# Gates as tanh, the decay loaded in its own layout, sums of squares added up on TensorE

## The chip, the cores and the metric

The kernel runs on one core of a Trainium2 chip. Its engines work side by side, each on its own list of instructions in order: TensorE (PE, with its weight load PEld), VectorE (DVE), ScalarE (ACT), GpSimd (POOL) and SyncE (SP), which here only issues DMAs. The metric is the device time of one execution in microseconds (us), as the median of several runs.

## What is computed

One layer of a hybrid decoder on 1024 tokens of 1024 features in float32. A combined projection of the normalised input feeds three mixers (retention, Mamba-2 SSD, gated linear attention), whose outputs are merged by learned gates; an MLP follows. What the change touches:

```python
proj = h @ w_in                                  # h = rmsnorm(x); columns for all mixers and gates
# SSD, 8 chunks of 128 tokens, 16 heads of 64, state 128; a_cs = cumsum(a) in a chunk
l_mat  = exp(where(causal, a_cs[l] - a_cs[m], -inf))
y_diag = einsum(cb, l_mat, xs)                   # within the chunk
y_off  = einsum(cc, prev_states, exp(a_cs))      # from the chunks before
y = y_diag + y_off + x * d_skip
sy = group_rmsnorm(y * silu(sz), ssd_norm_w, 2)
...
g_ret, g_ssd, g_gla = split(sigmoid(mg + merge_b), 3)
merged = g_ret * ret_out + g_ssd * ssd_out + g_gla * gla_out
x = x + merged @ w_out
```

## The kernel before

Large products are made of matmuls of 128 x 128 weights with 128 x 512 activations. Each float32 operand is split in a high part and a remainder (`whi` by a cast on ScalarE, line 156, `wlo` by a subtraction on VectorE, line 157), and `acc3` (line 159) adds three products for each pair, its matmul being line 164. Most products use a seven-product block scheme: `run_set` makes a set of weights out of seven units of 12 matmuls, with `us` (lines 360, 366) as partial results. Of the 34 sets of the combined projection the last 12 are the merge gates. `e_gate` (line 481) takes a finished bank of them, adds the partial result if there is one (line 486, VectorE), applies the sigmoid with the bias column `mb_c` (line 487, ScalarE) and stores the gate to DRAM (line 489, SyncE).

The mixers run between the units of these sets: `merge` (line 949) takes a unit from the sets, then as many mixer steps as are due. Nine gate sets, 63 units, are woven with the four `ssd_mixer` runs (line 686) of 8 chunks each, 32 chunks and 72 steps in all. The call is line 1041; it runs from about 565 to 840 us. The order in which each engine's list ends up is set by the framework's scheduler, which places instructions as their inputs and buffers come free.

A chunk of the SSD mixer has two stages. `load_in` (line 697) fetches the conv outputs `xin` (line 699) and the cumulated decays `ab`, spread over all partitions (line 701), one chunk ahead. `stage_a` transposes `xin` on TensorE (lines 713 to 715), makes `xs` and `xd` (lines 718 on) and the masked scores `cbm` (line 726) on VectorE and `bt` on ScalarE (line 724). The inter-chunk decay `eb` is the exponential of `ab`, picked out by head in two halves of 64 partitions (line 732), for every chunk but the first. Four Relus (line 734) and an exponential (line 736) on ScalarE and a product on VectorE (line 737) make the intra-chunk decay. `stage_b` forms the skip product `y` on GpSimd (line 745), multiplies on TensorE (lines 750, 754, 758), sums up on VectorE (lines 767 to 771, with `eb` at 769), stores `y` (line 772), squares it on ScalarE (line 774) and adds its two halves on GpSimd (line 775). `stat` (line 777), two chunks later, sums the squares over the partitions by a one-column fp32 matmul with ones (line 779) and copies the result to `ssq` (line 780). `ssd_rows` then makes the scales out of `ssq` (GpSimd power, line 177) and transposes them (line 805).

The short-lived tiles `xs`, `xd`, `eb`, `y` and `ysq` share one ring of nine buffers, `w1m` (line 704). Later, `load_o` (line 1064) loads the mixers' outputs and scales them by the norm weights `nw_c` (lines 1077, 1081), and `branch_part` (line 1090) multiplies them by the output weights and the product by the loaded gate (line 1107), 48 times, before the branches are added up.

Of the kernel before, what the change touches and what calls it, by code (L numbers as in the profile page):

```python
# [10 lines left out]
F32 = mybir.dt.float32  # L11
F32R = mybir.dt.float32r
I32 = mybir.dt.int32
AF = mybir.ActivationFunctionType
ALU = mybir.AluOpType
# [3 lines left out]
P = 128  # L19
# [7 lines left out]
SH, SP, SG = 16, 64, 2  # L27
# [84 lines left out]
def block_kernel(ctx, tc, i, out):  # L112
    nc = tc.nc
    V, S, G, PE = nc.vector, nc.scalar, nc.gpsimd, nc.tensor

    const = ctx.enter_context(tc.tile_pool(name="const", bufs=1))
# [15 lines left out]
    nw_c = cols[:, 0:16]  # L132
    mb_c = cols[:, 16:40]
# [3 lines left out]
    nw2_c = cols[:, 62:70]  # L137
    d_c = cols[:, 70:78]
    cw_c = [cols[:, 78 + 12 * j:90 + 12 * j] for j in range(4)]
    nhalf = const.tile([P, 16], F32, name="nhalf")  # L140
    V.memset(nhalf, -0.5)

# [338 lines left out]
    def e_gate(b, d0):  # L481
        def emit(n, par, ps, other):
            d = d0 + n
            r = ev.tile([P, 512], F32, name="gt", tag="w2k")
            if other is not None:
                V.tensor_tensor(out=r, in0=ps, in1=other, op=ALU.add)
            S.activation(out=r, in_=ps if other is None else r, func=AF.Sigmoid,
                         bias=mb_c[:, 8 * b + d:8 * b + d + 1])
            nc.sync.dma_start(out=gate_d[b][d].rearrange("p (j q t) -> q p j t", q=2, t=P)[par],
                              in_=r.rearrange("p (j t) -> p j t", t=P))  # L490
        return emit
# [194 lines left out]
    def ssd_mixer(g, f4):  # L686
        R = SH // SG // 2
# [9 lines left out]
        def load_in(c):  # L697
            xin = sp.tile([P, 6, P], F32, name="xin", bufs=3)
            nc.sync.dma_start(out=xin, in_=st_d[g][c][:, 4 * f4:4 * f4 + 6])
            ab = sp.tile([P, R, P], F32, name="ab", bufs=3)  # L700
            nc.sync.dma_start(out=ab, in_=acs_d[c * SH + h0:c * SH + h0 + R, :].partition_broadcast(P))
            ins[c] = xin, ab

        def w1m(name, shape):
            return sp.tile(shape, F32, name=name, tag="w1m", bufs=9)

        def stage_a(c):
            if c + 1 < NT:
                load_in(c + 1)
            xin, ab = ins.pop(c)  # L710
            pt = ptp.tile([P, 512], F32, name="tp", tag="tp")
            for j in range(2):
                PE.transpose(out=pt[:, j * P:(j + 1) * P], in_=xin[:, sx + j, :], identity=ident)
            PE.transpose(out=pt[:, 256:384], in_=xin[:, sb, :], identity=ident)
            PE.matmul(out=pt[:, 384:512], lhsT=xin[:, sb, :], rhs=xin[:, sb + 1, :], start=True, stop=True)
            ptv = pt[:, 0:256].rearrange("p (h d) -> p h d", h=R)
            xs = w1m("xs", [P, R, SP])
            V.tensor_tensor(out=xs, in0=ptv, in1=hb(dt, c), op=ALU.mult)
            xd = bt = eb = None
            if c + 1 < NT:  # L720
                xd = w1m("xd", [P, R, SP])
                V.tensor_tensor(out=xd, in0=ptv, in1=hb(dtd, c), op=ALU.mult)
                bt = sp.tile([P, P], F32, name="bt", bufs=2)
                S.copy(out=bt, in_=pt[:, 256:384])
            cbm = sp.tile([P, P], F32, name="cbm", bufs=2)
            V.tensor_tensor(out=cbm, in0=pt[:, 384:512], in1=tri, op=ALU.mult)
            if c > 0:
                eb = w1m("eb", [P, 2, P])
                av = ab.rearrange("p (k f) t -> p f k t", f=2)
                for f in range(2):  # L730
                    rs = slice(f * SP, (f + 1) * SP)
                    S.activation(out=eb[rs], in_=av[rs, f], func=AF.Exp)
            for h in range(R):
                S.activation(out=ab[:, h, :], in_=ab[:, h, :], func=AF.Relu, scale=-1.0,
                             bias=acs[:, c, h0 + h:h0 + h + 1])
            S.activation(out=ab, in_=ab, func=AF.Exp, scale=-1.0)
            V.tensor_tensor(out=ab, in0=ab, in1=cbm.unsqueeze(1).broadcast_to([P, R, P]), op=ALU.mult)
            live[c] = (xin, ab, xs, xd, bt, eb)

        def stage_b(c):  # L740
# [31 lines left out]
            nc.sync.dma_start(out=o_d[2 + g][c // 4][:, 2 * f4:2 * f4 + 2, c % 4, :], in_=y)  # L772
            sq = w1m("ysq", [P, 2, P])
            S.activation(out=sq, in_=y, func=AF.Square)
            G.tensor_tensor(out=sq[:, 0], in0=sq[:, 0], in1=sq[:, 1], op=ALU.add)

            def stat():
                ps = ptp.tile([P, 512], F32, name="tp", tag="tp")
                PE.matmul(out=ps[:, 0:1], lhsT=sq[:, 0], rhs=ones[:, 0:1], start=True, stop=True)
                V.tensor_copy(out=ssq[:, f4, g * NT + c:g * NT + c + 1], in_=ps[:, 0:1])  # L780
            return stat

# [281 lines left out]
    def load_o(h, res, order):  # L1064
        rsy = []
        for kt in order:
# [5 lines left out]
            nc.sync.dma_start(out=raw.rearrange("p (c t) -> p c t", c=4), in_=o_d[b][h][:, k])  # L1072
            hi = bp.tile([P, 512], F32R, name="ohi", tag="ohi", bufs=16)
            lo = bp.tile([P, 512], F32R, name="olo", tag="olo", bufs=16)
            nw = nw_c[:, kt:kt + 1]
            if b in (2, 3):
                V.scalar_tensor_tensor(out=raw, in0=raw, scalar=nw, in1=rsy[b - 2].rearrange("p c t -> p (c t)"),
                                       op0=ALU.mult, op1=ALU.mult)
# [11 lines left out]
    def branch_part(h, b, o, last=False):  # L1090
        first = (0, 4, 12)[b]
        ws = None
        for d in range(KD):
# [10 lines left out]
                c0 = n * P + (512 * (d % 2) if b != 1 else 0)  # L1104
                pairs.append(((ws[0][:, c0:c0 + P], ws[1][:, c0:c0 + P]), o[k]))
            acc3(ps, pairs)
            V.tensor_tensor(out=gt, in0=ps, in1=gt, op=ALU.mult)
            if b == 0:
                accs[d] = gt
            else:  # L1110
# [268 lines left out]
```

## Time and profile before

| | |
|---|---|
| runs | 1908.94, 1909.88, 1905.97 us; median 1908.94 |
| profiled execution | 1909.4 us; span from first to last instruction 1907.6 us |
| busy in the span | PE 1866.1 us, DVE 1175.6, ACT 892.7, POOL 199.9 |
| mean granted TensorE clock | 0.993 of full speed |
| SSD stretch, 565 to 840 us | PE 264.29 of 275.00 us, ACT 233.37, DVE 196.43 |

The profile is of one execution. Busy time counts an engine's instructions; an engine's standing time is put down to the instruction that it waited for. The granted clock is that of TensorE alone: 1.00 is 2.4 GHz, 0.50 is 1.2 GHz, and what lies between is a mean over a stretch with both.

### The profile page before, as it was taken

Reading aid. Unit: us, or ns where it says so; the run is one execution under the profiler, and the core shown is the slowest. Engines: PE = TensorE matmul, PEld = TensorE weight load, DVE = VectorE, ACT = ScalarE, POOL = GpSimd, SP = SyncE. Lnnn points to the kernel's source line nnn. Section 1 sums busy time; section 2 is a strip of 40 time slices with the busy share of each in tenths; the row PEclk is TensorE's granted clock in tenths of the full one; section 3 lists DMA queues with packets and bytes.
Section 4 is the critical chain, followed back from the end, with each engine's and each line's share of the span. In section 5 each row is a group of like instructions: output and inputs, shape, how many; then the busy total and the mean of one; then the engine's idle time right before and its main releaser. Section 6 shows DMA issues by size and latency. Waiting matters only on the chain. (4 is left out here: it accounts for less than half of the span.)

```text
span 1907.6 us, 25681 instructions
## 1 busy us (share of the span) xinstructions
PE 1866.1 (98%) x9396; PEld 1538.6 (81%) x9396; DVE 1175.6 (62%) x1921; ACT 892.7 (47%) x1568; POOL 199.9 (10%) x247
## 2 busy tenths in 40 slices
PE   8999999999999999999899999999999999999998
PEld 8977778888887777777788989988888888888886
DVE  6867767668557677765877456584555434444444
ACT  7522333345449879876764123454444422111213
POOL 0011100001211112211322031000000000000003
PEclk9999999999999999999999999999999999999999
DMA  6434434234655555538667543542323362332222
GB/s 213 148 113 147 128 105 127 89 111 146 192 176 157 150 170 162 174 96 300 195 209 270 187 155 124 208 166 94 122 99 110 122 231 90 104 94 89 91 73 90
DMA packets 179342, 278.03 MB, mean 146 GB/s; under 512 B 13168, under 2 KB 114576, under 8 KB 172560
## 3 DMA queue, kind: packets, MB, share of 16 engines
q1 hardware_dynamic: 178640, 275.48, 45.4%
q8 instruction: 74, 1.21, 0.3%
q10 hardware_dynamic: 576, 0.92, 0.1%
q14 instruction: 52, 0.43, 0.1%
HBM read 193.43 MB, written 78.72 MB: 143 GB/s over the span
## 5 line engine op out<-in xcount | busy, mean ns | idle before, releaser
L156 ACT CAST whi<-raw 128x1024 fp32r<-128x1024 f32 (+1 forms) x230 | 240.6, 1048 | 494.2 <-PE mm L164 464.1
L157 DVE TENSOR_TENSOR wlo<-raw,whi 128x1024 fp32r<-128x1024 f32 (+1 forms) x230 | 293.8, 1278 | 130.6 <-ACT whi L156 123.4
L164 PE MATMUL mm<-ht,whi 128*128 128x512 f32 x1104 | 353.9, 401 | 2.5 <-DVE us L360 2.5
L164 PEld LDWEIGHTS mm<-ht,whi 128*128 128x128 f32 x1104 | 206.0, 189 | 52.8 <-DVE us L360 4.2
L164 PE MATMUL mm<-ht,wlo 128*128 128x512 f32 x552 | 219.7, 399 | 0.0
L164 PE MATMUL mm<-whi,al 128*128 128x512 f32 x512 | 202.5, 396 | 0.0
L164 PE MATMUL mm<-whi,ah 128*128 128x512 f32 x512 | 202.5, 395 | 0.0
L164 PE MATMUL mm<-wlo,ah 128*128 128x512 f32 x512 | 202.5, 395 | 0.0
L1323 DVE TENSOR_TENSOR x<-mm,x 128x512 f32<-128x512 f32 x128 | 88.2, 689 | 159.2 <-PE mm L164 159.2
L164 PE MATMUL mm<-he,whi 128*128 128x512 f32 x560 | 182.7, 404 | 0.2
L164 PE MATMUL mm<-ht,w 128*128 128x512 f32 x552 | 138.2, 397 | 0.0
L164 PEld LDWEIGHTS mm<-ht,wlo 128*128 128x128 f32 x552 | 104.1, 189 | 25.0
L164 PEld LDWEIGHTS mm<-he,whi 128*128 128x128 f32 x560 | 104.9, 190 | 23.9 <-ACT us L366 0.3
L164 PEld LDWEIGHTS mm<-ht,w 128*128 128x128 f32 x552 | 103.2, 188 | 24.6
L360 DVE TENSOR_TENSOR us<-mm,us 128x512 f32<-128x512 f32 x92 | 63.4, 689 | 90.7 <-PE mm L164 90.4
L164 PEld LDWEIGHTS mm<-whi,al 128*128 128x128 f32 x512 | 96.2, 188 | 23.4
L164 PEld LDWEIGHTS mm<-whi,ah 128*128 128x128 f32 x512 | 96.2, 188 | 23.3
L164 PEld LDWEIGHTS mm<-wlo,ah 128*128 128x128 f32 x512 | 96.2, 188 | 23.2
L164 PE MATMUL mm<-he,wlo 128*128 128x512 f32 x280 | 111.8, 399 | 0.0
L164 PE MATMUL mm<-ohi,whi 128*128 128x512 f32 x256 | 102.9, 403 | 2.7 <-ACT ohi L1081 2.7
L164 PE MATMUL mm<-ohi,wlo 128*128 128x512 f32 x256 | 102.0, 398 | 0.0
L164 PE MATMUL mm<-olo,whi 128*128 128x512 f32 x256 | 102.0, 398 | 0.0
(287 smaller groups left out, 3549.1 us busy)
## 6 DMA issues: line engine op xcount, KB each, us to landing
raw<-w_in SPq DMA_DIRECT2D x34, 1024.0 KB, 5.3
raw<-w_o SPq DMA_DIRECT2D x32, 512.0 KB, 4.0
raw<-w_up SPq DMA_DIRECT2D x16, 1024.0 KB, 5.0
act<-rl SPq DMA_DIRECT2D x64, 256.0 KB, 2.0
raw<-w_down SPq DMA_DIRECT2D x32, 512.0 KB, 4.3
araw<-act SPq DMA_DIRECT2D x64, 256.0 KB, 3.3
gate<-gt SPq DMA_DIRECT2D x48, 256.0 KB, 3.6
xin<-st SPq DMA_DIRECT2D x32, 384.0 KB, 3.5
```

The lines of the kernel that those rows point to most:

```text
L156: S.copy(out=dst_hi, in_=src)
L157: V.tensor_tensor(out=dst_lo, in0=src, in1=dst_hi.bitcast(F32), op=ALU.subtract)
L164: PE.matmul(out=ps, lhsT=l, rhs=r, start=(first and j == 0), stop=(last and j == n - 1), skip_group_check=open_)
L360: V.tensor_tensor(out=t, in0=ps, in1=other, op=ALU.add)
L1323: V.tensor_tensor(out=xs, in0=ps, in1=xs, op=ALU.add)
```

## The change

It has three parts. The gates are kept as tanh of half the biased value instead of the sigmoid; as the sigmoid of z is half of 1 + tanh(z/2), the merge multiplies by (gate + 1), and the factor of one half goes into the norm weights `nwh`. The inter-chunk decay is no longer picked out of `ab` but loaded by two DMAs of its own, 64 x 2 x 128 each, straight into the layout in which it is used, in three buffers of its own; its exponential is then one instruction in place, and the shared ring `w1m` has six buffers instead of nine. The squares' two halves are no longer added on GpSimd: `stat` runs two matmuls that add up in PSUM.

```diff
@@ -137,6 +137,10 @@
     nw2_c = cols[:, 62:70]
     d_c = cols[:, 70:78]
     cw_c = [cols[:, 78 + 12 * j:90 + 12 * j] for j in range(4)]
+    mbh = const.tile([P, 24], F32, name="mbh")
+    V.tensor_scalar(out=mbh, in0=mb_c, scalar1=0.5, scalar2=None, op0=ALU.mult)
+    nwh = const.tile([P, 16], F32, name="nwh")
+    V.tensor_scalar(out=nwh, in0=nw_c, scalar1=0.5, scalar2=None, op0=ALU.mult)
     nhalf = const.tile([P, 16], F32, name="nhalf")
     V.memset(nhalf, -0.5)
 
@@ -484,8 +488,8 @@
             r = ev.tile([P, 512], F32, name="gt", tag="w2k")
             if other is not None:
                 V.tensor_tensor(out=r, in0=ps, in1=other, op=ALU.add)
-            S.activation(out=r, in_=ps if other is None else r, func=AF.Sigmoid,
-                         bias=mb_c[:, 8 * b + d:8 * b + d + 1])
+            S.activation(out=r, in_=ps if other is None else r, func=AF.Tanh, scale=0.5,
+                         bias=mbh[:, 8 * b + d:8 * b + d + 1])
             nc.sync.dma_start(out=gate_d[b][d].rearrange("p (j q t) -> q p j t", q=2, t=P)[par],
                               in_=r.rearrange("p (j t) -> p j t", t=P))
         return emit
@@ -699,15 +703,21 @@
             nc.sync.dma_start(out=xin, in_=st_d[g][c][:, 4 * f4:4 * f4 + 6])
             ab = sp.tile([P, R, P], F32, name="ab", bufs=3)
             nc.sync.dma_start(out=ab, in_=acs_d[c * SH + h0:c * SH + h0 + R, :].partition_broadcast(P))
-            ins[c] = xin, ab
+            eb = None
+            if c > 0:
+                eb = sp.tile([P, 2, P], F32, name="eb", bufs=3)
+                av = acs_d[c * SH + h0:c * SH + h0 + R, :].rearrange("(k f) t -> f k t", f=2)
+                for f in range(2):
+                    nc.sync.dma_start(out=eb[f * SP:(f + 1) * SP], in_=av[f].partition_broadcast(SP))
+            ins[c] = xin, ab, eb
 
         def w1m(name, shape):
-            return sp.tile(shape, F32, name=name, tag="w1m", bufs=9)
+            return sp.tile(shape, F32, name=name, tag="w1m", bufs=6)
 
         def stage_a(c):
             if c + 1 < NT:
                 load_in(c + 1)
-            xin, ab = ins.pop(c)
+            xin, ab, eb = ins.pop(c)
             pt = ptp.tile([P, 512], F32, name="tp", tag="tp")
             for j in range(2):
                 PE.transpose(out=pt[:, j * P:(j + 1) * P], in_=xin[:, sx + j, :], identity=ident)
@@ -716,7 +726,7 @@
             ptv = pt[:, 0:256].rearrange("p (h d) -> p h d", h=R)
             xs = w1m("xs", [P, R, SP])
             V.tensor_tensor(out=xs, in0=ptv, in1=hb(dt, c), op=ALU.mult)
-            xd = bt = eb = None
+            xd = bt = None
             if c + 1 < NT:
                 xd = w1m("xd", [P, R, SP])
                 V.tensor_tensor(out=xd, in0=ptv, in1=hb(dtd, c), op=ALU.mult)
@@ -725,11 +735,7 @@
             cbm = sp.tile([P, P], F32, name="cbm", bufs=2)
             V.tensor_tensor(out=cbm, in0=pt[:, 384:512], in1=tri, op=ALU.mult)
             if c > 0:
-                eb = w1m("eb", [P, 2, P])
-                av = ab.rearrange("p (k f) t -> p f k t", f=2)
-                for f in range(2):
-                    rs = slice(f * SP, (f + 1) * SP)
-                    S.activation(out=eb[rs], in_=av[rs, f], func=AF.Exp)
+                S.activation(out=eb, in_=eb, func=AF.Exp)
             for h in range(R):
                 S.activation(out=ab[:, h, :], in_=ab[:, h, :], func=AF.Relu, scale=-1.0,
                              bias=acs[:, c, h0 + h:h0 + h + 1])
@@ -772,11 +778,11 @@
             nc.sync.dma_start(out=o_d[2 + g][c // 4][:, 2 * f4:2 * f4 + 2, c % 4, :], in_=y)
             sq = w1m("ysq", [P, 2, P])
             S.activation(out=sq, in_=y, func=AF.Square)
-            G.tensor_tensor(out=sq[:, 0], in0=sq[:, 0], in1=sq[:, 1], op=ALU.add)
 
             def stat():
                 ps = ptp.tile([P, 512], F32, name="tp", tag="tp")
-                PE.matmul(out=ps[:, 0:1], lhsT=sq[:, 0], rhs=ones[:, 0:1], start=True, stop=True)
+                for k in range(2):
+                    PE.matmul(out=ps[:, 0:1], lhsT=sq[:, k], rhs=ones[:, 0:1], start=(k == 0), stop=(k == 1))
                 V.tensor_copy(out=ssq[:, f4, g * NT + c:g * NT + c + 1], in_=ps[:, 0:1])
             return stat
 
@@ -1072,7 +1078,7 @@
             nc.sync.dma_start(out=raw.rearrange("p (c t) -> p c t", c=4), in_=o_d[b][h][:, k])
             hi = bp.tile([P, 512], F32R, name="ohi", tag="ohi", bufs=16)
             lo = bp.tile([P, 512], F32R, name="olo", tag="olo", bufs=16)
-            nw = nw_c[:, kt:kt + 1]
+            nw = nwh[:, kt:kt + 1]
             if b in (2, 3):
                 V.scalar_tensor_tensor(out=raw, in0=raw, scalar=nw, in1=rsy[b - 2].rearrange("p c t -> p (c t)"),
                                        op0=ALU.mult, op1=ALU.mult)
@@ -1104,7 +1110,7 @@
                 c0 = n * P + (512 * (d % 2) if b != 1 else 0)
                 pairs.append(((ws[0][:, c0:c0 + P], ws[1][:, c0:c0 + P]), o[k]))
             acc3(ps, pairs)
-            V.tensor_tensor(out=gt, in0=ps, in1=gt, op=ALU.mult)
+            V.scalar_tensor_tensor(out=gt, in0=gt, scalar=1.0, in1=ps, op0=ALU.add, op1=ALU.mult)
             if b == 0:
                 accs[d] = gt
             else:
```

Line numbers of the changed kernel are higher by 4 up to `load_in` and by up to 10 behind it: 487 becomes 491, 732 becomes 738, 734 becomes 740, 736 becomes 742, 750 becomes 756, 774 becomes 780, 779 becomes 785. Three places show how instructions move.

ScalarE at the first gates of the SSD stretch, before (`gt` is a gate, `eb` and `ab` the decays, `whi` a weight's high part):

```order
L734 ACTIVATE ab<-ab,acs 128x128 x4
L724 COPY bt<-tp 128x128
L736 ACT_TABLE_LOAD
L736 ACTIVATE ab<-ab 128x512
L487 ACT_TABLE_LOAD
L487 ACTIVATE gt<-mm,k_cols 128x512
L724 COPY bt<-tp 128x128
L732 ACT_TABLE_LOAD
L732 ACTIVATE eb<-ab 64x256 x2
L734 ACTIVATE ab<-ab,acs 128x128 x4
L156 CAST whi<-raw 128x1024
L736 ACTIVATE ab<-ab 128x512
```

The same place with the change (line 491 is the gate, 738 the inter-chunk decay):

```order
L740 ACTIVATE ab<-ab,acs 128x128 x4
L734 COPY bt<-tp 128x128
L742 ACT_TABLE_LOAD
L742 ACTIVATE ab<-ab 128x512
L491 ACTIVATE gt<-mm,mbh 128x512
L738 ACTIVATE eb<-eb 128x256
L740 ACTIVATE ab<-ab,acs 128x128 x3
L734 COPY bt<-tp 128x128
L740 ACTIVATE ab<-ab,acs 128x128
L160 CAST whi<-raw 128x1024
L742 ACTIVATE ab<-ab 128x512
L738 ACTIVATE eb<-eb 128x256
```

The table loads between gates and exponentials are gone but for one, and the two half exponentials are one of 128 x 256; in the whole program 76 table loads become 11.

TensorE at one of the sums of squares, before (line 750 starts a chunk's `stage_b`; `mm` is a bank of the gate sets, `tp` the sum):

```order
L750 MATMUL mx<-ab,xs 64x128 x4
L754 MATMUL mx<-xin,sst 128x128 x2
L758 MATMUL mx<-xd,bt 128x256
L164 MATMUL mm<-ht_198,wlo 128x512
L779 MATMUL tp<-ones,ysq 128x1
L164 MATMUL mm<-he_191,whi 128x512
L750 MATMUL mx<-ab,xs 64x128 x4
L754 MATMUL mx<-xin,sst 128x128 x2
```

TensorE at the same chunks with the change:

```order
L168 MATMUL mm<-he_195,whi 128x512
L168 MATMUL mm<-he_196,whi 128x512
L168 MATMUL mm<-he_195,wlo 128x512
L785 MATMUL tp<-ones,ysq 128x1 x4
L168 MATMUL mm<-ht_202,whi 128x512
L168 MATMUL mm<-ht_203,whi 128x512
L785 MATMUL tp<-ones,ysq 128x1 x2
L168 MATMUL mm<-ht_202,wlo 128x512
```

Before, a sum of squares stands one matmul behind a chunk's `stage_b`; with the change the sums stand in pairs of matmuls behind a full unit of 12, of which the last three rows are shown.

SyncE in the same stretch, before (`gate_..<-gt` stores a gate, `raw` loads weights, `o_..<-y` stores a chunk's output):

```order
L772 DMA o_0_132<-y 128x2x128
L699 DMA xin<-st_99 128x768
L701 DMA ab<-acs_d 128x512
L489 DMA gate_0_112<-gt 512x1x128
L772 DMA o_0_132<-y 128x2x128
L699 DMA xin<-st_99 128x768
L701 DMA ab<-acs_d 128x512
L772 DMA o_0_132<-y 128x2x128
L699 DMA xin<-st_99 128x768
```

SyncE with the change (line 711 loads the decay):

```order
L778 DMA o_0_136<-y 128x2x128
L703 DMA xin<-st_103 128x768
L705 DMA ab<-acs_d 128x512
L493 DMA gate_7_115<-gt 512x1x128
L711 DMA eb<-acs_d 64x2x128 x2
L778 DMA o_0_136<-y 128x2x128
L703 DMA xin<-st_103 128x768
L705 DMA ab<-acs_d 128x512
L711 DMA eb<-acs_d 64x2x128
L778 DMA o_0_136<-y 128x2x128
L703 DMA xin<-st_103 128x768
```

The decay's loads stand among the loads of `xin` and `ab` and the stores of the chunks; SyncE's list grows from 693 to 725 rows, equal neighbours in one row.

## Rows read from the trace of the kernel before

**Rows 1.** The page's busy times: us (share of the span) x instructions.

```profile
PE 1866.1 (98%) x9396; PEld 1538.6 (81%) x9396; DVE 1175.6 (62%) x1921; ACT 892.7 (47%) x1568; POOL 199.9 (10%) x247
```

**Rows 2.** Windows: length, busy us (count) of each engine, PEclk, DMA share, GB/s.

```profile
300.00:400.00 100.00, 100.00 (x430) 80.33 (x429) 71.48 (x87) 38.63 (x44) 0.00 (x0) 1.00 0.33 102
470.00:565.00 95.00, 93.96 (x548) 80.85 (x548) 51.78 (x115) 45.95 (x140) 24.57 (x28) 1.00 0.61 180
565.00:840.00 275.00, 264.29 (x1439) 207.84 (x1438) 196.43 (x420) 233.37 (x416) 56.85 (x89) 0.98 0.54 160
```

**Rows 3.** TensorE's waits, 565 to 840 us: total us, times, longest us.

```profile
PE tp L779 <- POOL ysq L775: 5.2, 3, 2.6
PE tp L713 <- DMA xin<-st: 1.5, 3, 1.2
```

**Rows 4.** Timeline around 632 us: start, us, engine, operation [idle <-releaser].

```profile
627.04 1.28 ACT L732 ACT_TABLE_LOAD   x1
...
630.95 0.42 ACT L774 ACTIVATE ysq<-y 128x256 f32<-128x256 f32 x1 [0.46 <-DVE y L771]
...
631.45 0.45 POOL L775 TENSOR_TENSOR ysq<-ysq 128x128 f32<-128x128 f32 x1 [4.58 <-ACT ysq L774]
...
631.96 0.38 PE L779 MATMUL tp<-ones,ysq 128*128 128x1 f32 x2 [2.57 <-POOL ysq L775]
```

**Rows 5.** Groups by shape, 560-850 us: xcount | busy, mean ns | idle.

```profile
L487 ACT ACT_TABLE_LOAD x29 | 37.2, 1283 | 0.5
...
L732 ACT ACT_TABLE_LOAD x20 | 25.7, 1283 | 0.3
...
L732 ACT ACTIVATE eb<-ab 64x256 f32<-64x256 f32 x56 | 23.3, 415 | 0.9
...
L736 ACT ACT_TABLE_LOAD x9 | 11.5, 1283 | 0.2
...
L779 PE MATMUL tp<-ones,ysq 128*128 128x1 f32 x64 | 9.3, 217 | 5.3 <-POOL ysq L775 5.2
```

**Rows 6.** Windows, columns as in rows 2, after the two long waits.

```profile
630.00:640.00 10.00, 7.70 (x33) 5.75 (x33) 6.09 (x13) 5.97 (x14) 0.78 (x2) 0.83 0.51 132
690.00:705.00 15.00, 12.57 (x50) 9.26 (x48) 8.58 (x20) 12.06 (x28) 2.67 (x5) 0.77 0.46 128
```

**Rows 7.** Groups by shape, 830 to 1130 us, columns as in rows 5.

```profile
L1107 DVE TENSOR_TENSOR gt<-mm,gt 128x512 f32<-128x512 f32 x41 | 28.2, 688 | 26.8 <-PE mm L164 22.6 <-DMA raw<-w_o 2.1 <-POOL gt L1111 1.8
...
L1077 DVE SCALAR_TENSOR_TENSOR oraw<-oraw,k_cols,rsy 128x512 f32<-128x512 f32 x16 | 11.8, 746 | 1.5 <-DMA oraw<-o 1.3
```

**Rows 8.** Timeline at the start, VectorE.

```profile
5.81 0.16 DVE L236 TENSOR_SCALAR vsx<-ssx 128x1 f32<-128x1 f32 x1 [4.78 <-ACT xsq L234]
```

**Rows 9.** TensorE's timeline around a sum of squares, columns as in rows 4.

```profile
597.12 0.40 PE L164 MATMUL mm<-ht,wlo 128*128 128x512 f32 x1
597.36 0.28 PE L779 MATMUL tp<-ones,ysq 128*128 128x1 f32 x2
597.49 0.71 PE L164 MATMUL mm<-ht,whi 128*128 128x512 f32 x2
598.04 0.40 PE L164 MATMUL mm<-ht,wlo 128*128 128x512 f32 x1
...
598.74 0.39 PE L164 MATMUL mm<-ht,wlo 128*128 128x512 f32 x1
```

**Rows 10.** DMA, 565-840 us: packets, MB, share; KB, us to landing.

```profile
q1 hardware_dynamic: 38784, 43.80, 53.7%
...
ab<-acs_d SPq DMA_DIRECT2D x32, 256.0 KB, 3.5
```

**Rows 11.** TensorE's waits, 840 to 900 us, columns as in rows 3.

```profile
PE mm L164 <- ACT ohi L1081: 2.7, 1, 2.7
PE tp L805 <- POOL rs_r L177: 0.7, 1, 0.7
```

**Rows 12.** SyncE's timeline: one issue, columns as in rows 4.

```profile
601.48 0.32 SPq L701 DMA_DIRECT2D ab<-acs_d  x1
```

## The prediction

> **What bounds the kernel now.** I read the busy shares first, then the stretches, then the waits of TensorE inside the stretch that the change touches. TensorE is busy for 98% of the span [rows 1], so only two things can move the time: fewer or more matmuls, and the 2% in which TensorE stands or runs at a low clock. The change lives in the SSD stretch (565 to 840 us). There TensorE is busy for 264.29 of 275.00 us, so it stands for 10.7 us; ScalarE is busy for 233.37 us (85%), VectorE for 196.43 us (71%). Two stretches serve as a yardstick [rows 2]: at 300 to 400 us, with ScalarE at 39% and VectorE at the same 71%, TensorE never stands; at 470 to 565 us, where the retention chunks are woven in and ScalarE is at 48%, it stands for 1.04 of 95 us. So a full VectorE alone does not make it wait; what sets the SSD stretch apart is ScalarE.
>
> The waits say the same. Half of the 10.7 us is the sum-of-squares matmul of line 779 waiting for GpSimd's addition of line 775 (5.2 us in three waits); the rest is in smaller pieces, among them 1.5 us on the loads of the next chunk [rows 3]. Followed back, the wait at 631.96 us is ScalarE's: a table load at 627.04 and the exponentials behind it push the square to 630.95, GpSimd's addition (it had idled 4.58 us for it) to 631.45, and TensorE stands for 2.57 us [rows 4]. ScalarE spends 37.2 us on 29 table loads for the gates and 25.7 us on 20 for line 732, and nine more of the same 1283 ns stand at line 736: 58 loads, 74 us [rows 5].
>
> TensorE pays a second time. In the 10 us after 630 the granted clock is 0.83 on average, in the 15 us after 690 it is 0.77, that is, part of each stretch at the lower level of 1.2 GHz; both follow a wait at line 779 [rows 6]. With TensorE busy for 7.70 and 12.57 us there, the loss is 7.70 x 0.17 + 12.57 x 0.23 = 4.2 us. The page "TensorE: Matmul & The Clock Gate" of the Trainium skill (section "What's actually happening") says that the throttled state is the default and activity releases it; by that the loss goes when the waits go. Were it the narrow 64-column SSD matmuls instead, which stay, the 4.2 us would stay too and the sum would end 4 us later; the stretches agree with the first reading, since the same matmuls run at full clock wherever TensorE has not stood.
>
> **Part 1, the gates.** The sigmoid becomes a tanh of the half argument. In the order of ScalarE shown above, the exponentials and the gates now follow each other without a load: 58 loads in the SSD stretch become one, 57 x 1.283 = 73 us of ScalarE. The exponential of the inter-chunk decay falls from 56 instructions of 415 ns [rows 5] to 28 of about the same length (twice the rows, same row length): 28 x 0.415 = 11.6 us. ScalarE goes from 233 to about 149 us of 275, or 54%: near the 48% of the 470-565 stretch. So I give the SSD stretch that stretch's share of standing time: 1.04 / 95 x 275 = 3.0 us, a gain of **7.7 us** (bounds: 10.7, if it is as tight as 300 to 400; 0, if the waits have other causes). With the long waits the low clock goes: **4.0** of the 4.2 us (bounds 0 and 4.2).
>
> The price stands in the merge: VectorE's product of gate and branch becomes (gate + 1) x branch, a three-operand form. Today's product takes 688 ns; the nearest form with a scalar and two tensors takes 746 ns [rows 7]. 48 x 0.058 = 2.8 us of VectorE, which has waited for TensorE for most of its idle time there: hidden, 0 on the path (bound 2.8). The two small halving instructions at the start come before VectorE's first use at 5.81 us, where it had idled 4.78 us [rows 8]; they have to wait for the columns, but even so fit: 0 (bound 0.3, two such instructions).
>
> **Part 2, the sums of squares.** GpSimd's 32 additions go, and with them one hop in the chain of [rows 4] (0.45 us at 631.45). In their place line 785 runs a second fp32 matmul per chunk on TensorE, the bound engine, so each counts in full. An fp32 matmul is two passes in the trace. A triple of 512-column matmuls usually takes 0.70 us (from 598.04 to 598.74); the one with a sum of squares inside took 0.92 (597.12 to 598.04): 0.22 us each [rows 9]. 32 x 0.22 = **+7.0 us**. Bounds: 32 x 0.13 = 4.2 us, if only the step from its own start at 597.36 to the next matmul's start at 597.49 counts, and 9.3 us, the busy time of today's 32 [rows 5]. I take 7.0, since it is a difference of two complete triples. In the new order the pair also stands behind a full 12-matmul unit and works on a square of an older chunk, so I expect it to wait for nothing; this is part of the 7.7.
>
> **Part 3, the decay by DMA.** 56 more transfers of 64 KB go through SyncE's queue, two for each of 28 chunks, ahead of the next chunk's loads. One of today's 256 KB loads lands 3.5 us after issue [rows 10], and each is issued a chunk (275 / 32 = 8.6 us) ahead. In engine time: the queue's 38784 packets took 53.7% of 16 engines over 275 us, or 61 ns each; 56 x 128 packets add 27 us, so that the share grows by 0.10 (by bytes alone by 0.05): 0.54 to 0.64, and the 470-565 stretch runs at 0.61 with hardly a wait [rows 2, 10]. I book 0, with rival (b) for the other case. The page "DMA: Bandwidth & Descriptors" of the Trainium skill (section "Measured (HBM→SBUF, 128 partitions, SWDGE, issued from GpSimd)") speaks against this part: it gives 0.95 us for 64 KB, 32% of the peak, and wants transfers batched to 1 MiB. An estimate from that page is 56 x 0.95 = 53 us, a share of 0.18 more instead of 0.10, about 0.72; no row here shows such a load.
>
> The shared ring of work buffers goes from nine slots to six, as the decay leaves it. By it the skip product on GpSimd (line 751) has to wait until the same chunk's matmuls have read an earlier slot, and VectorE's sum behind it waits in turn. Today the product is done long before its use, and VectorE works on that chunk only after the same matmuls: 0 (bound: rival (a)).
>
> **Around 840 to 890 us.** After the SSD stretch ScalarE still has gates of the last set, each behind a table load, ahead of the scaled retention outputs, and the projection out of the mixers waits 2.7 us for these [rows 11]. Two fewer loads ahead would cover it nearly (2 x 1.283 = 2.6); I expect 2.0 back. Against it, the row of final scales (0.7 us of waiting at line 805) now starts behind three double sums of squares instead of one single: +0.6. Together **-1.4** (bounds -2.7 and +1).
>
> **Sum**, against the profiled execution of 1909.4 us: -7.7 - 4.0 + 7.0 - 1.4 = -6.1, or 1903.3 us. The median of the runs (1908.94) lies 0.5 below the profiled execution, so the forecast for the median is **1902.8 us**.
>
> **Rivals.**
> (a) *The waits come back under another name.* With six slots the chain GpSimd product, VectorE sum, square is tied closer to TensorE, and VectorE at 71% with a latency chain of five instructions per chunk is what is late next. Speaks for it: VectorE is the second busiest engine and its idle time is mostly waiting for others. Against: the 470-565 stretch. Then 7 us of standing remain and 2 us of low clock: -3.7 - 2.2 + 7.0 - 1.4 = -0.3, so about 1908.6. Chance 0.25.
> (b) *Slower by the queue.* SyncE works in order; an issue costs it 0.32 us (601.48 us in the trace [rows 12]), and a decay load that waits for its buffer holds the next chunk's inputs back, on which today's transposes already wait now and then (1.5 us in three waits [rows 3]). Exposed in full it costs 28 x 0.64 = 18 us, so about 1920.7. It eats the gain from 6.1 / 28 = 0.22 us per chunk, and makes the kernel slower by more than 0.2% from 0.35 us. Against it: the loads run a chunk ahead. Chance 0.07.
> (c) *The relief does not reach TensorE.* ScalarE gets faster, but the waits at 565 to 840 keep their length because they are ordered by VectorE, and only the added matmuls count: 1909.4 + 7.0 - 0.5 = 1915.9. Against it: the chain in [rows 4], which runs through ScalarE. Chance 0.07.
> (d) *Better:* no standing at all and the cheap end of the added matmuls: -10.7 - 4.2 + 4.2 - 2.7 = -13.4, so about 1895.5. Chance 0.06.
> My forecast, with residual standing between 0 and 5 us and the matmuls between 4.2 and 9.3, spans 1897 to 1906.5 and has 0.55.
>
> **How the numbers follow.** A measurement of this kernel tells about 0.2% from no change, or 3.8 us: faster is below 1905.1, slower above 1912.7. Faster holds 0.49 of the forecast's 0.55, all of (d) and 0.03 of (a): 0.58. Same holds 0.06 of the forecast and 0.21 of (a): 0.27. Slower holds (b), (c) and 0.01 of (a): 0.15. The range from 1896.5 to 1910.5 covers the forecast and nearly all of (a) and leaves out (b), (c) and most of (d), 2 in 10.
>
> **What would show it.** In the SSD stretch: ScalarE near 150 of 275 us and one table load where there were 58; TensorE standing about 3 us and no granted clock below 0.95 between 565 and 840; matmuls of line 785 at 128 instead of 64 records; no wait of TensorE for a square. A wait of line 756 or 723 of several us in total would speak for (a), one on the loads of line 703 or 711 for (b). The forecast is wrong if the standing time stays above 7 us, or if one more sum of squares costs clearly more than 0.22 us.

## The result: faster by 0.8%, more than twice what was forecast

| | before | changed |
|---|---|---|
| median of the runs | 1909.41 us (4 runs, 1905.97 to 1910.78) | 1893.83 us (4 runs, 1893.12 to 1896.00) |
| profiled execution, span | 1907.6 us | 1890.7 us |
| TensorE's standing time in the span | 41.5 us | 31.7 us |

The ratio is 0.9923, with a 95% interval of 0.9906 to 0.994. The direction was right; 15.6 us came where 6.1 had been summed up, and the time lies below the range.

The page of the changed kernel begins so (columns as in [rows 1]):

```profile
PE 1859.0 (98%) x9460; PEld 1543.9 (82%) x9460; DVE 1176.0 (62%) x1923; ACT 796.1 (42%) x1475; POOL 185.2 (10%) x215
```

64 more matmul records, two for each of 32 added matmuls; ScalarE has lost 97 us. The windows of the changed kernel, with the stretches of [rows 2] and [rows 6] and two behind the SSD stretch (columns as in [rows 2]):

```profile
300.00:400.00 100.00, 100.00 (x432) 81.08 (x431) 72.31 (x88) 38.94 (x44) 0.00 (x0) 1.00 0.33 103
470.00:565.00 95.00, 93.64 (x541) 80.43 (x541) 52.13 (x112) 45.42 (x140) 23.57 (x28) 1.00 0.61 179
565.00:840.00 275.00, 270.14 (x1521) 215.76 (x1520) 202.83 (x429) 154.83 (x341) 44.09 (x57) 1.00 0.59 173
835.00:860.00 25.00, 25.00 (x104) 19.13 (x103) 15.53 (x29) 18.48 (x23) 0.00 (x0) 1.00 0.69 226
...
860.00:1160.00 300.00, 291.06 (x1634) 248.50 (x1633) 200.11 (x415) 133.25 (x349) 67.24 (x70) 1.00 0.63 205
630.00:640.00 10.00, 10.00 (x56) 8.45 (x55) 7.00 (x14) 5.99 (x12) 0.62 (x1) 1.00 0.52 145
690.00:705.00 15.00, 14.86 (x84) 11.60 (x82) 10.02 (x19) 8.63 (x18) 0.61 (x1) 1.00 0.74 223
```

The same two stretches of the kernel before:

```profile
835.00:860.00 25.00, 24.23 (x87) 16.12 (x86) 14.62 (x29) 18.67 (x23) 3.37 (x2) 0.86 0.30 83
...
860.00:1160.00 300.00, 287.54 (x1576) 242.70 (x1575) 197.08 (x413) 141.56 (x356) 65.47 (x68) 1.00 0.65 213
```

In the SSD stretch TensorE now stands for 4.9 us instead of 10.7, with ScalarE at 155 of 275 us, and the granted clock is 1.00 wherever it had been lower, at 835 to 860 us too, where before it was 0.86 on average (25 x 0.14 = 3.5 us). TensorE's waits of the changed kernel from 565 to 840 us (columns as in [rows 3]):

```profile
PE tp L723 <- DMA xin<-st: 2.8, 4, 1.4
PE tp L811 <- POOL rs_r L181: 1.0, 1, 1.0
PE tp L723 <- DMA ab<-acs_d: 0.9, 1, 0.9
```

The wait for the sum of squares [rows 3] is gone; what is left is mostly on the inputs of the next chunk. The wait for the scaled retention outputs [rows 11] is gone as well. The groups of the changed kernel that answer to [rows 5], 560 to 850 us:

```profile
L785 PE MATMUL tp<-ones,ysq 128*128 128x1 f32 x128 | 16.1, 233 | 0.2
...
L738 ACT ACTIVATE eb<-eb 128x256 f32<-128x256 f32 x28 | 11.6, 414 | 16.0 <-DMA eb<-acs_d 15.8
...
L742 ACT ACT_TABLE_LOAD x1 | 1.3, 1283 | 0.0
```

**Where the 16.9 us of span went.** Standing time gave 9.8 us (5.8 at 565 to 840, 0.8 at 835 to 860, 3.5 at 860 to 1160). Time lost to the low clock, added up as the width times one minus the granted clock over stretches of 5 us (the last, incomplete one left out), fell from 12.0 to 3.8 us: 8.2. The added matmuls cost 7.0, by the price that [rows 9] gave and that a run below bears out. That makes 11.0; 5.9 us remain. About half of them can be seen in stretches that the change does not touch: there TensorE goes through the same matmuls at another pace. ScalarE's copies of the first product of two sets that follow each other, in the kernel before and then in the changed one (timeline of ScalarE: start, us, line, operation):

```profile
372.77 0.59 ACT L366 COPY us<-mm 128x512 f32<-128x512 f32 x1 [2.41 <-PE mm L164]
...
392.37 0.59 ACT L366 COPY us<-mm 128x512 f32<-128x512 f32 x1 [0.37 <-PE mm L164]
```

```profile
371.92 0.59 ACT L370 COPY us<-mm 128x512 f32<-128x512 f32 x1 [2.40 <-PE mm L168]
...
391.44 0.59 ACT L370 COPY us<-mm 128x512 f32<-128x512 f32 x1 [0.36 <-PE mm L168]
```

A set takes 19.60 us before and 19.52 with the change, at a granted clock of 1.00 and without a wait in both; most sets from 74 to 451 us take these times. From the first such copy to the twentieth it is 376.5 us before (74.66 to 451.17) and 375.3 with the change (74.74 to 450.00), 1.2 us less. In the last stage the output additions run from 1545.5 to 1901.1 us before and from 1530.1 to 1884.2 with the change, 355.6 against 354.1 us. Eleven sets of the MLP between 1270 and 1500 us gain another 0.4. So some 3 of the 5.9 us are seen as pace; the rest was found by subtraction alone, lies where the instructions stand in another order, and its cause is open.

### The profile page after: what moved, and what is told of

Read it like the earlier page. It is cut to its first block, busy times and chain, and to the rows that moved or that the text cites. A ratio compares the mean times of both kernels' runs of the same rounds, so it can differ in the third digit from the quotient of the medians.

```text
span 1890.7 us, 25783 instructions
## 1 busy us (share of the span) xinstructions
PE 1859.0 (98%) x9460; PEld 1543.9 (82%) x9460; DVE 1176.0 (62%) x1923; ACT 796.1 (42%) x1475; POOL 185.2 (10%) x215
```

## The experiments

Times are medians; the kernel before, run beside each, had 1909.0 to 1910.7 us. First the three parts of the change, alone and undone.

**Gates alone.** Of the diff only the gates, their columns and the merge.

> The kernel before with the gates as tanh and nothing else. Theory (the table loads were what TensorE paid for, in standing time, in the low clock and in the waits behind the SSD stretch; the second matmul per chunk costs 7 us): about 1891, that is the changed kernel less its 7 us for the matmuls plus a few us for the waits that the sums of squares on GpSimd may still bring; ScalarE loses about 65 table loads. Rival (the decay's own load carries the gain, since it takes work and a dependence off ScalarE): no better than 1903.

Measured: **1887.2 us**, ratio 0.9878 (0.9864 to 0.9891). The gates alone bring more than the whole change. The SSD stretch of this run:

```profile
565.00:840.00 275.00, 271.90 (x1488) 215.48 (x1487) 210.54 (x439) 174.32 (x378) 61.21 (x89) 1.00 0.55 167
```

TensorE stands for 3.1 us, the very 3.0 that the prediction had booked for the sum of all parts, at full clock; its standing at line 779 is gone although GpSimd still adds.

**The addition put back.** The changed kernel with

```diff
             S.activation(out=sq, in_=y, func=AF.Square)
+            G.tensor_tensor(out=sq[:, 0], in0=sq[:, 0], in1=sq[:, 1], op=ALU.add)
...
-                for k in range(2):
-                    PE.matmul(out=ps[:, 0:1], lhsT=sq[:, k], rhs=ones[:, 0:1], start=(k == 0), stop=(k == 1))
+                PE.matmul(out=ps[:, 0:1], lhsT=sq[:, 0], rhs=ones[:, 0:1], start=True, stop=True)
```

> The changed kernel with the two halves of the squares added on GpSimd again and one matmul per chunk. Theory (a sum of squares costs TensorE 0.22 us, in full): 32 x 0.22 = 7 us faster than the changed kernel, about 1887. Rival (the second matmul hides behind weight loads or standing time, 0.11 us): about 1890. Second rival (GpSimd's addition brings the wait back): no faster than the changed kernel, 1894 or more.

Measured: **1892.1 us**, 1.7 less than the changed kernel. This is none of the three theories alone: the matmuls are saved, but some of the waits return. Its SSD stretch, and its first two waits there:

```profile
565.00:840.00 275.00, 265.38 (x1463) 209.80 (x1462) 205.17 (x432) 156.96 (x344) 65.50 (x89) 1.00 0.61 175
```

```profile
PE tp L785 <- POOL ysq L781: 3.2, 2, 2.5
PE tp L723 <- DMA xin<-st: 3.2, 4, 1.4
```

9.6 us of standing against 4.9: 4.8 of the 7 are given back. With the decay's loads and six shared buffers GpSimd's addition is late again; without them, in the gates alone, it is not.

**Two matmuls alone.** The kernel before with the same lines the other way round.

> The kernel before with two matmuls per sum of squares instead of GpSimd's addition, nothing else. Theory: +7 us for the matmuls, up to 5 us back for the waits on GpSimd's addition and the low clock behind them, which ScalarE's lateness mostly keeps: 1911 to 1916. Rival (the addition on GpSimd was the cause of the waits and the low clock): 1907 or less.

Measured: **1912.0 us**, ratio 1.0008 (0.9999 to 1.0017): as expected. By itself this part brings nothing, and the interval leaves open whether it costs. The wait stays and has another name (3.3 us for the square on ScalarE itself): GpSimd's addition had only passed ScalarE's lateness on.

**The decay's loads alone.** The kernel before with the load, the one exponential and six buffers.

> The kernel before with the decay loaded in its own layout (and six shared buffers), nothing else. Theory: ScalarE is relieved of 12 us and of some table loads at the decay, so a few us better, 1903 to 1909. Rival (the loads in SyncE's queue hold the inputs of the next chunk back): 1912 or more, with waits on the loads of the next chunk.

Measured: **1898.5 us**, ratio 0.9938 (0.9925 to 0.9952), better than either theory. Two windows of this run:

```profile
565.00:840.00 275.00, 265.98 (x1465) 209.69 (x1464) 197.92 (x426) 216.66 (x389) 62.05 (x89) 1.00 0.61 175
835.00:860.00 25.00, 25.00 (x103) 18.97 (x103) 14.39 (x26) 23.54 (x27) 0.00 (x0) 1.00 0.60 201
```

TensorE still stands for 9.0 us, hardly less than before, and still 66 table loads are made; but the clock is 1.00 in both stretches, which in the kernel before lost 5.2 + 3.5 us. A loss of 1.7 us stands at 890 to 895 us instead. So some 7 of these 11 us are the clock.

**The decay's loads undone.** The changed kernel with the decay picked out of `ab` again and nine shared buffers, so that gates and two matmuls remain.

> The changed kernel with the decay picked out of the scores' rows again (two halves on ScalarE, nine shared buffers): gates and two matmuls. Theory (with the gates as tanh the decay's loads bring nothing more): the gates alone plus 32 x 0.22 = 7 us, 1893 to 1895, no different from the changed kernel. Rival (the decay's loads hold TensorE up, by SyncE's queue or the six buffers): faster than the changed kernel, 1890 or less. Second rival (they carry a gain of their own, as alone on the kernel before): 1900 or more.

Measured: **1895.1 us**, as expected: with the gates in place the decay's loads bring nothing that can be measured. Against the gates alone it is 7.9 us slower: 32 more matmuls at 0.22 us are 7.0, and most of its early sets run at the slower pace of 19.60 us. The pair of matmuls in the changed kernel's timeline (TensorE) says the same:

```profile
824.55 0.39 PE L168 MATMUL mm<-he,wlo 128*128 128x512 f32 x1
824.79 0.39 PE L168 MATMUL mm<-he,whi 128*128 128x512 f32 x1
825.02 0.50 PE L785 MATMUL tp<-ones,ysq 128*128 128x1 f32 x4
825.38 0.48 PE L168 MATMUL mm<-he,whi 128*128 128x512 f32 x1
825.69 0.40 PE L168 MATMUL mm<-he,wlo 128*128 128x512 f32 x1
```

From 824.55 to 825.69 are 1.14 us for three large matmuls and the pair, 0.44 over the usual 0.70, twice the 0.22 of [rows 9].

**Loads or buffers?** Why do the decay's loads cost 5 us where GpSimd adds (1892.1 against 1887.2)? The same kernel as with the addition put back, but the decay's tile taken from the shared ring, which is nine deep again:

```diff
-                eb = sp.tile([P, 2, P], F32, name="eb", bufs=3)
+                eb = w1m("eb", [P, 2, P])
...
-            return sp.tile(shape, F32, name=name, tag="w1m", bufs=6)
+            return sp.tile(shape, F32, name=name, tag="w1m", bufs=9)
```

> Gates as tanh and the decay by its own loads, one matmul with GpSimd's addition, as in the run that puts the addition back, but the decay lies in the shared ring, which has nine buffers again. Theory (the six buffers tie GpSimd, VectorE and TensorE together, and bring the 5 us by which that run stays behind the gates alone): 1887 to 1888. Rival (it is the loads in SyncE's queue): 1891 to 1893, with waits for the next chunk's loads.

Measured: **1892.0 us**, no different, so the six buffers do not bring the 5 us. They may bear a part of the standing: with nine, TensorE waits 0.6 us for GpSimd's addition instead of 3.2 and stands for 7.9 us instead of 9.6, while the profiled execution lost almost 4 us more to a low clock. TensorE's first waits in the SSD stretch of this run:

```profile
PE tp L723 <- DMA xin<-st: 3.0, 4, 1.3
PE tp L811 <- POOL rs_r L181: 1.3, 1, 1.3
PE tp L723 <- DMA ab<-acs_d: 1.0, 1, 1.0
```

Against the gates alone (1.7 us for `xin`, none for `ab`) the chunk's inputs come later. Part of the delay comes after the issue: a load of `xin` lands 4.0 us after its issue (median) in the changed kernel and in the runs with these loads (4.1 in the one with nothing else), and 3.4 to 3.5 in the kernel before, the gates alone and the gates with two matmuls. What SyncE's list adds was not told apart. The decay's loads themselves land after 3.4 us in the changed kernel. The share of the DMA engines grew from 0.55 to 0.61, by 0.06, near the 0.05 by bytes and not the 0.10 by packets.

**Which loads hurt?** The gates alone again, with tanh up to the end of the SSD stretch and the sigmoid in the last two sets, and then the mirror image.

```diff
-            S.activation(out=r, in_=ps if other is None else r, func=AF.Tanh, scale=0.5,
-                         bias=mbh[:, 8 * b + d:8 * b + d + 1])
+            S.activation(out=r, in_=ps if other is None else r, func=AF.Tanh if (b != 2 or d < 4) else AF.Sigmoid,
+                         scale=0.5 if (b != 2 or d < 4) else 1.0,
+                         bias=(mbh if (b != 2 or d < 4) else mb_c)[:, 8 * b + d:8 * b + d + 1])
```

> The gates alone, as tanh up to the end of the SSD stretch; the last two gate sets keep the sigmoid and its table loads (the merge then multiplies by twice the gate). Theory (the loads behind the SSD stretch cost on their own: 3.4 us of low clock at 840 to 855 us and 2.7 us of waiting for the scaled retention outputs): some 6 us slower than the gates alone, 1893, with a granted clock below 1.00 behind the last sum of squares. Rival (these costs were late effects of the SSD stretch): 1887 to 1888.

> The mirror image: the sigmoid with its loads in the SSD stretch, tanh in the last two gate sets only. Theory: the SSD stretch keeps its 10 us of standing and 5 us of low clock; 3.4 + 2.7 us come back behind it, and up to 3 us by the place of the weights: 1901 to 1904. Rival (all of it is the SSD stretch): 1907 to 1910.

Measured: **1886.5 us** with tanh in the SSD stretch alone, no worse than with all gates as tanh: there the theory fell. Measured: **1903.6 us** for the mirror image, within what was expected, but not for its reason. Two windows of the mirror image:

```profile
565.00:840.00 275.00, 264.59 (x1443) 208.78 (x1441) 197.21 (x421) 235.14 (x418) 58.82 (x89) 0.98 0.53 160
835.00:860.00 25.00, 24.20 (x100) 17.05 (x100) 13.55 (x25) 19.14 (x23) 3.07 (x2) 1.00 0.36 107
```

The low clock at 835 to 860 is absent in both, and the wait for the scaled retention outputs is still there in the mirror image (3.2 us) and absent in the other. So the table loads behind the SSD stretch are not what causes that wait: it goes with the loads in place and stays without them. The low clock at 835 to 860 goes with several unrelated edits, but not always for good. In the mirror image a loss of the same size stands behind that wait:

```profile
880.00:890.00 10.00, 7.52 (x19) 5.64 (x20) 5.84 (x10) 4.39 (x10) 0.29 (x2) 0.66 0.91 306
```

The gates alone have 0.83 in the same 10 us; the kernel before, the changed kernel and the run with tanh in the SSD stretch alone have 1.00.

**The pace.** Next, whether TensorE's pace comes from where the tiles lie: the two new columns, 96 + 64 bytes per partition, push all tiles behind them, the weights among them, by 160 bytes, and leave the activations, which are allotted from the other end, where they are. An unused tile in the kernel before does the same with the same instructions:

```diff
+    pad = const.tile([P, 40], F32, name="pad")
+    V.memset(pad, 0.0)
     nhalf = const.tile([P, 16], F32, name="nhalf")
```

> The kernel before, with one unused tile of 160 bytes per partition where the change has its two halved columns: the same instructions in the same order but for one fill at the start, and every tile behind it, the weights among them, 160 bytes further. Theory (the pace of TensorE in stretches that the change does not touch, 19.52 against 19.60 us per set, hangs on where the weights lie): 19.52 us per set and some 4 us less, about 1905.5. Rival (the pace belongs to the gates as tanh, or to chance): 19.60 us and 1909.5.

> The kernel before, with an unused tile of 64 bytes per partition in the same place: the weights keep their place within 64 bytes, which the 160 bytes change by 32. Theory (what counts is the place within 64 bytes, between weights and activations): 19.60 us per set as before, 1909.5. Rival (any shift changes it): 19.52 us or another number, about 1905.

In the timeline, two sets with 160 bytes and then with 64:

```profile
370.99 0.59 ACT L368 COPY us<-mm 128x512 f32<-128x512 f32 x1 [2.40 <-PE mm L166]
...
390.51 0.59 ACT L368 COPY us<-mm 128x512 f32<-128x512 f32 x1 [0.34 <-PE mm L166]
```

```profile
372.20 0.59 ACT L368 COPY us<-mm 128x512 f32<-128x512 f32 x1 [2.41 <-PE mm L166]
...
391.81 0.59 ACT L368 COPY us<-mm 128x512 f32<-128x512 f32 x1 [0.37 <-PE mm L166]
```

19.52 and 19.6 us, as the theories say. The times, **1908.5 and 1908.2 us** (ratios 0.9985, 0.9975 to 0.9994, and 0.9989, 0.998 to 0.9998), do not tell the two apart: the profiled run with 160 bytes happened to lose 15.9 us to the low clock, where the kernel before lost 12.0 with the same instructions.

The gates without a shift (the columns halved in their own place) and the same with 32 bytes:

> The gates alone as tanh, with the two columns halved in their own place, so that no tile moves. Theory (the shift gives 4 us of the gates' gain): 19.60 us per set, about 1891, against 1887.2 for the gates with their own tiles. Rival (the tanh itself brings the pace): 19.52 us per set, 1887.

> The gates alone, halved in place, with an unused tile of 32 bytes per partition ahead of the other tiles: the instructions of the gates without a shift and one fill, the weights moved by 32 bytes. Theory (the place of the weights within 64 bytes sets the pace; 160 bytes moved it by 32, 64 bytes did not): 19.52 us per set in most sets, 2.79 us per output tile in the last stage, and 1 to 4 us less than without the shift, 1885 to 1888. Rival (the 160 bytes worked in another way, by a whole row of 128 or by the order of the tiles): 19.60 and 2.80 us, 1889.

Measured: **1888.9 us** without a shift, between the two theories, at 19.60 us per set. The shift of 160 bytes was worth 1.7 us in the medians. In the profiled executions it was 1.5 us of span, although the one with the shift lost 1.7 us more to the low clock: together about 3 us, as much as was seen in the stretches that the change does not touch. With 32 bytes: **1870.0 us**, ratio 0.9786 (0.9771 to 0.98). Two of its sets:

```profile
366.42 0.59 ACT L370 COPY us<-mm 128x512 f32<-128x512 f32 x1 [2.32 <-PE mm L168]
...
385.46 0.59 ACT L370 COPY us<-mm 128x512 f32<-128x512 f32 x1 [0.21 <-PE mm L168]
```

19.04 us. Neither theory had that. The weights (`whi`, `wlo`, `w`) begin at 192 of each 256 bytes in the kernel before, at 96 in the changed kernel, at 0 with 64 bytes, and at 224 with 32 bytes; the activations (`ht`, `he`, `hb`) begin at 224 in all of these. No view of the profile shows these places; what the runs show by themselves is how far the tiles were moved. Four runs more followed this up:

> The changed kernel with an unused tile of 128 bytes per partition behind its two columns: same instructions but one fill, the weights at 224 of each 256 bytes, where the activations lie (the changed kernel: 96, the kernel before: 192). Theory (TensorE's pace hangs on the places of weights and activations within 256 bytes, and the change moved the weights by 160): 19.04 us per set, some 17 us less than the changed kernel, about 1877. Rival (32 bytes worked in the other run by something of the gates' own halving in place): 19.52 us, 1894.

> The kernel before with an unused tile of 32 bytes per partition, nothing else: the weights at 224 of 256 as the activations. Theory (place): 19.04 us per set and 17 to 19 us less, about 1891. Rival (the gain needs the gates as tanh): 19.60 us and 1909.

> The gates alone, halved in place, with an unused tile of 32 bytes on the side of the activations: the activations go from 224 to 192 of 256 bytes, the weights stay at 192. Theory A (what counts is that both have the same place): 19.04 us per set, about 1870. Theory B (the weights or the activations have to be at 224): 19.60 us per set, 1889.

> The gates alone, halved in place, with an unused tile of 288 bytes, so that the weights have moved by 32 and another 256. Theory (only the place within 256 bytes counts): 19.04 us per set and the same time as with 32 bytes, 1870. Rival (the place within 512 bytes counts too): another pace, faster or slower than 19.04.

| kernel | weights, activations (of 256) | us per set | median | ratio (interval) |
|---|---|---|---|---|
| kernel before | 192, 224 | 19.60 | 1909.4 | |
| changed kernel | 96, 224 | 19.52 | 1893.8 | 0.9923 (0.9906 to 0.994) |
| changed kernel + 128 bytes | 224, 224 | 19.04 | 1874.2 | 0.9812 (0.9798 to 0.9827) |
| kernel before + 32 bytes | 224, 224 | 19.04 | 1891.7 | 0.9896 (0.988 to 0.9913) |
| gates + 32 bytes on the other side | 192, 192 | 19.04 | 1868.7 | 0.9784 (0.9768 to 0.9799) |
| gates + 288 bytes | 224, 224 | 19.04 | 1869.5 | 0.9788 (0.9774 to 0.9803) |

Two sets of the run in which only the activations were moved:

```profile
365.67 0.59 ACT L371 COPY us<-mm 128x512 f32<-128x512 f32 x1 [2.32 <-PE mm L166]
...
384.71 0.59 ACT L371 COPY us<-mm 128x512 f32<-128x512 f32 x1 [0.21 <-PE mm L166]
```

Theory A holds: it is the place of the one side against the other within 256 bytes. Equal is fast, half of 256 apart a little better than 32 apart. Each edit moved all tiles behind it on its side; that it is the weights and the activations among them is argued from what TensorE reads, not tested tile by tile. With equal places the change is worth 1891.7 - 1874.2 = 17.5 us, and the gates alone, at 1869 to 1870, beat the changed kernel there by 4 to 6 us and the kernel before as it was by 2.2%. That is the best version found.

## Why the prediction was wrong

**What held.** ScalarE was behind the waits: the gates alone, with GpSimd's addition and the shared ring left as they were, brought TensorE's standing at 565 to 840 us to 3.1 us where 3.0 were forecast. It is this run that shows it; in the row itself the square last waited for VectorE's sum (0.46 us [rows 4]). The matmuls of the sums of squares cost 7.0 us, in the pair's timeline and in the difference of two kernels (7.9 in the medians). The halving at the start and the three-operand product in the merge stayed off the path (line 1113 takes 683 ns on average, not more than the 688 of [rows 7]). The ring of six cost no time that the medians show.

**The low clock, 4.0 us in the sum, was 8.2.** This is the first mis-sized term. I counted the two episodes that follow a wait at line 779 [rows 6] and left out the third, at 835 to 860 us, with 3.5 us. The two also lost 5.2 us and not 4.2: I weighed the windows by TensorE's busy time, but most of the standing in them comes before the clock falls (in the first the wait ends at 632 us, and the clock from 632.8 to 636.2 is 0.50). The wait ahead of the third episode is short (0.67 us at 842.00), and the sum has no term for the clock behind it; the episode is absent at that place in every edit of the three parts above, though some of these runs have a low clock later, between 880 and 980 us. What decides is still open: with the addition put back, TensorE stood for 2.5 us at 690 to 705 us without any loss of clock,

```profile
690.00:705.00 15.00, 12.54 (x73) 9.81 (x70) 9.18 (x20) 7.16 (x14) 1.07 (x2) 1.00 0.72 194
```

while the kernel before, with almost the same busy time there (12.57 us), had 0.77 [rows 6]. By the page of the Trainium skill ("TensorE: Matmul & The Clock Gate", "What's actually happening") activity releases the throttle. The clock of 1.00 from 300 to 400 us, where TensorE never stands, agrees with that; why one of these two stretches lost and the other did not, no run here shows. The loss also differs between executions of one kernel: 15 executions of the kernel before had mean granted clocks from 0.990 to 0.995. So some of the 8.2 us can be luck. The changed kernel's profile lost 3.8, nearly all of it at the start.

**The pace, about 3 of the 5.9 us left over, had no term at all.** The sum went through the instructions that the change adds and removes; that the two new columns move the weights of every matmul in the program by 160 bytes does not show in that view, and I did not compare the places. The runs on the pace showed that they matter. That the shift went the right way was luck. How much of the 15.6 us it is: some 3 us by the stretches that the change does not touch and by the gates with and without shift in the profiles, 1.7 in the medians of the latter. The other 3 us or so are a remainder whose cause stays open.

**Waits behind the SSD stretch, 1.4 us in the sum, were 4.3** (0.8 at 835 to 860 and 3.5 at 860 to 1160). I had the 2.7 us for the retention outputs right, but gave the chunks of the gated linear attention nothing, where TensorE had stood for ScalarE's copies 4.9 us; in the changed kernel it is 3.1 us.

**The decay's loads, booked at 0, were 2 us of standing against it.** The standing in the SSD stretch came to 4.9 us and not 3.0; without these loads (gates and two matmuls) it was 2.6, though that kernel as a whole was not faster (1895.1 us). That is rival (b) in small: the waits are on the inputs of the next chunk. Alone on the kernel before they gained 11 us, most of it clock losses that the gates remove anyway: the parts alone give -22, -11 and +2, and together -16. The page "DMA: Bandwidth & Descriptors" of the Trainium skill (section "Measured (HBM→SBUF, 128 partitions, SWDGE, issued from GpSimd)") had spoken against small transfers. The waits agree in the sign; but the share grew by 0.06, a third of the 0.19 that my estimate from that page gives (53 of 275 us; I wrote 0.18).

So the terms in the order of the sum were -5.8 (forecast -7.7), -8.2 (-4.0), +7.0 (+7.0), -4.3 (-1.4) and -5.9 (0): -17.2, where the spans differ by 16.9; the 0.3 are small changes of standing elsewhere. The 5.9 is what was left over, so that the terms add up is no check on it. The range ended at 1896.5 because no rival was better than 1895.5, and that one had the standing, the matmuls and the wait behind the stretch at their best, but the third episode of low clock and the pace at nothing.

## What to carry to other kernels

Before a change is judged, compare a stretch that it does not touch: if the same instructions take another time there, something else moved, and here it was the address of the weights against that of the activations, worth more than the change. Price every episode of low clock in the trace, not only those behind the wait that the change removes, and expect parts that remove the same episodes not to add up. Work that two engines can do (here an addition on GpSimd or a second matmul) belongs on the engine that has time: with the gates alone changed, TensorE did not wait for GpSimd's addition, and the matmuls cost 7 us.

## What the runs showed of the hardware

- The pace of back-to-back 128x512 matmuls of this kernel hangs on how far the tiles on one side of a partition, the weights among them, are moved against those on the other, the activations among them: 19.04 us per set of 84 matmuls (227 ns each) if weights and activations have the same place within 256 bytes, 19.52 us (232 ns) in most sets if they are 128 apart, 19.60 us (233 ns) if they are 32 apart, at a granted clock of 1.00 in all. Adding 256 bytes more changed nothing. Only these distances were tried, and why it is so was not tested. One kernel with 128 bytes between them (gates and two matmuls) ran most early sets at 19.60 and the later ones at the faster pace.
- The loss to a low granted clock differs between executions of one kernel: 15 executions of the kernel before had mean granted clocks from 0.990 to 0.995, at 1907.1 to 1912.7 us. The profiles of the kernel before with an unused tile of 160 or 64 bytes lost 15.9 and 15.4 us to it where the kernel before lost 12.0, with the same instructions but for one fill.
